# Row-major attention order, a new order of the mixing steps, and GELU as one operation

## The chip, the cores and the metric

One core of a Trainium2 chip runs the whole kernel. The metric is the device time of one execution in microseconds (us), as the median of several runs. The engines of the core are TensorE (PE, with its weight loads shown apart as PEld), VectorE (DVE), ScalarE (ACT), GpSimd (POOL) and SyncE (SP), which issues the DMAs.

## What is computed

Two layers of an encoder over 512 tokens, which form a grid of 8 rows and 64 columns, with 1024 channels in float32:

```python
h = rmsnorm(x, g_mix[l]); z = h @ w_in[l]                  # 1024 -> 2560
q, k, v, x_rec, gate = split(z)                            # 512 channels each
att = neighbourhood_attention(q, k, v, rel_bias[l])        # 8 heads of 64
xc = depthwise_conv(x_rec, width 4)
rec = (rg_lru(xc, forward) + rg_lru(xc, backward)) * gelu(gate, approximate=True)
x = x + concat(rmsnorm(att), rmsnorm(rec)) @ w_out[l]
h = rmsnorm(x, g_ffn[l]); a, b = split(h @ w_up[l])        # 1024 -> 2 x 3072
x = x + (gelu(depthwise_conv(a, width 3)) * b) @ w_down[l] # then, at the end, a last rmsnorm
```

In the attention each token sees all 8 rows and a window of 16 columns around its own column, clamped at the grid's edge, with a learned bias for each relative offset, and a softmax over these 128 keys. `rg_lru` has two gate products per direction (64x64 blocks), a decay exp(-8 r softplus(-lam)) and a linear scan over the tokens.

## The kernel before

Activations lie with channels on the 128 partitions and the 512 tokens along the free dimension. Each float32 matrix product is made of three passes over halves that are rounded to fp32r (`mm3`, L187 to L190): hi x hi, lo x hi, hi x lo. Weights arrive in chunks of 128x1024 (L157); ACT makes the hi half (L171), DVE the lo half (L172), three chunks ahead of their use. A column of the input projection, 128 output channels, is 24 matmuls of 128x512 (`column_parts`, L209).

A layer has a mixing stage and an MLP stage. The mixing stage begins with the four tiles of `x_rec` (L442) and then follows the list MIX (L43), whose steps are: q, k, v, g, one column of the projection with its evacuation (query_tile, key_tile, value_tile, gate_tile), where a and b are its halves; c, the convolution of a tile; t, the gate products of a tile with decay and scans (`lru_gates`, 12 matmuls and a long chain on ACT and DVE); u, the transposes of a value tile to token order, with copies of it moved by 64 partitions that POOL writes to `edge` (L564); S, T, P for each pair of heads and half of the grid's columns; o, parts of the output projection; n, the statistics of both norms. S, T and P have numbers 0 to 7: number n is head pair n // 2 and column half n % 2.

S (`scores`, L603) multiplies four blocks of queries, each 8 grid columns by 8 rows for two heads, with the keys of 16 or 24 grid columns: four float32 matmuls into two PSUM banks, then the bias and the maximum (L622), exp with its sum (L628) and the division (L632). T (`transposes`, L639) turns the probabilities into two banks and splits them in hi and lo (L653, L654). P (`products`, L657) multiplies by the values into one bank and copies the result into `att` (L679).

The program's text gives every instruction a place. The framework's scheduler then orders each engine's instructions: by modelled time it takes, of those that are ready, the one that stands first, and `with urgent()` (L141) moves instructions ahead of all that are not urgent. The order on each engine is fixed when the kernel is built. In the kernel before, scores and transposes are urgent as a whole (L724, L727), their matmuls too.

Tokens of a tile in attention stand in column order: by grid column, and the 8 rows of a column side by side. So a query, key or value tile is evacuated with a step of 8 elements on one side (L528, L536, L547), and the attention's result is copied back with a step of 64 (L679). A query tile is a pair of tiles, in each of which the part of the other head is zero (POOL, L517).

The pools that matter: `p_t` with 12 slots of 128x512 for most temporaries, `p_h` with 24, three PSUM banks for columns and gate products (`ps_mm`), two for scores (`ps_s`), two for transposes (`ps_pt`), one for products (`ps_o`; the fourth bank of a gate step until the first product has used it, L479).

Of the kernel before, what the change touches and what calls it, by code (L numbers as in the profile page):

```python
# [9 lines left out]
F32 = mybir.dt.float32  # L10
# [4 lines left out]
P = 128  # L15
# [24 lines left out]

MIX = ("q0 c0 c1 k0 t0 k1 q1 c2 t1 q2 k2 c3 t2 k3 q3 S0 v0a T0 t3 v0b g0a v1a S1 u0 P0 "  # L43
       "T1 g0b S2 v1b S3 g1a P1 u1 T2 v2a T3 P2 S4 S5 v2b g1b g2a T4 g2b P3 u2 P4 T5 S6 "
       "v3a v3b P5 g3a T6 S7 u3 o0 g3b P6 T7 o1 P7 o2 o3 o4 n o5 o6").split()
# [54 lines left out]
def encoder(ctx: ExitStack, tc: tile.TileContext, x_d, w_d, cols_d, bias_d, out_d):  # L100
# [153 lines left out]
    for t in edge:  # L254
        nc.gpsimd.memset(f32(t[0:64, 3 * P:T]), 0.0)
        nc.gpsimd.memset(f32(t[64:P, 0:P]), 0.0)

    NL = 16
    lam = cols[:, COLS["lru_lam"]:COLS["lru_lam"] + NL]
    sp = const.tile([P, NL], F32, name="sp")  # L260
# [79 lines left out]
    def by_column(ap):  # L340
        return ap.rearrange("p (c r) -> p r c", r=ROWS)

    def by_row(ap):
        return ap.rearrange("p (r c) -> p r c", r=ROWS)
# [82 lines left out]
    def layer(l, xn):  # L427
# [79 lines left out]
        qk = {}  # L507

        def query_tile(i):

            qk[i] = [big(p_h, "h", f"q{l}{i}{n}") for n in range(2)]

            def zones(other):
                return [by_head(t[64 * a:64 * a + 64])[:, :, a ^ other] for t in qk[i] for a in (0, 1)]

            for z in zones(1):
                nc.gpsimd.memset(z, 0.0)  # L517
            ps = psum(ps_mm, f"qps{l}{i}")
            yield from column_parts(ps, "w_in", l, i, xg, 4)
            with urgent():  # L520
                for n, z in enumerate(zones(0)):
                    rows = slice(64 * (n % 2), 64 * (n % 2) + 64)
                    cs = slice(32 * (n // 2), 32 * (n // 2) + 32)

                    def grid(ap):
                        return by_row(ap)[rows, :, cs].rearrange("p r (j c) -> p r j c", c=8)
# [12 lines left out]

        v = [None] * 4  # L540
# [29 lines left out]
        recs = [None] * 4  # L570
        atts = [None] * 4

        def gate_tile(t):
            ps = psum(ps_mm, f"gate{l}{t}")
            yield from column_parts(ps, "w_in", l, 16 + t, xg, 4)
            z = big(p_t, "t", f"z{l}{t}")
            with urgent():
                nc.vector.tensor_tensor(out=z, in0=ps, in1=rb, op=ALU.mult)
            s = big(p_t, "t", f"zs{l}{t}")
            nc.scalar.activation(s, z, AF.Square)  # L580
            nc.vector.tensor_scalar(out=s, in0=s, scalar1=0.044715, scalar2=1.0, op0=ALU.mult, op1=ALU.add)
            nc.vector.tensor_tensor(out=s, in0=s, in1=z, op=ALU.mult)
            nc.scalar.activation(s, s, AF.Tanh, scale=math.sqrt(2.0 / math.pi))
            nc.vector.scalar_tensor_tensor(out=z, in0=s, scalar=1.0, in1=z, op0=ALU.add, op1=ALU.mult)
            nc.vector.scalar_tensor_tensor(out=fb[t], in0=fb[t], scalar=0.5, in1=z, op0=ALU.mult, op1=ALU.mult)
# [16 lines left out]

        def scores(h):  # L603
            blocks = range(4 * (h % 2), 4 * (h % 2) + 4)
            bt, qt, kt = bias[h // 2], qk[h // 2][h % 2], qk[4 + h // 2]
            pr = {}
            st_ = probs_of[h % 2]
            mx = p_s.tile([P, 4], F32, tag="mx", name=f"mx{l}{h}")
            sm = p_s.tile([P, 4], F32, tag="sm", name=f"sm{l}{h}")
            for pair in (blocks[0:2], blocks[2:4]):  # L610
                ps = psum(ps_s, f"s{l}{h}{pair[0]}")
                o = 0
                for b in pair:
                    kc0, w, _ = BLOCKS[b]
                    nc.tensor.matmul(ps[:, o:o + ROWS * w], qt[:, b % 4 * P:(b % 4 + 1) * P],  # L615
                                     kt[:, ROWS * kc0:ROWS * (kc0 + w)], start=True, stop=True)
                    c0 = 0 if b % 2 else 2 * P - ROWS * w
                    pr[b] = st_[:, b % 4, c0:c0 + ROWS * w], ps[:, o:o + ROWS * w]
                    o += ROWS * w
                for b in pair:  # L620
                    _, w, bo = BLOCKS[b]
                    nc.vector.tensor_tensor_reduce(out=pr[b][0], in0=pr[b][1], in1=bt[:, bo:bo + ROWS * w], scale=1.0,  # L622
                                                   scalar=-3e38, op0=ALU.add, op1=ALU.max,
                                                   accum_out=mx[:, b % 4:b % 4 + 1])
                    pr[b] = pr[b][0]
            nc.vector.tensor_scalar(out=mx, in0=mx, scalar1=-1.0, scalar2=None, op0=ALU.mult)  # L626
            for b in blocks:
                nc.scalar.activation(pr[b], pr[b], AF.Exp, bias=mx[:, b % 4:b % 4 + 1],  # L628
                                     accum_out=sm[:, b % 4:b % 4 + 1])
            nc.vector.reciprocal(sm, sm)  # L630
            for b in blocks:
                nc.vector.tensor_scalar(out=pr[b], in0=pr[b], scalar1=sm[:, b % 4:b % 4 + 1], scalar2=None,  # L632
                                        op0=ALU.mult)
# [5 lines left out]
        def transposes(h, pr):  # L639
# [10 lines left out]
            sl = slice(n[0] * P, (n[-1] + 1) * P)  # L650
            t1, t2 = [[big(p_t, "t", f"pt{l}{h}{c}{a}", F32R) for a in range(2)] for c in range(2)]
            for t, src, cs in ((t1, whole, slice(0, T)), (t2, part, sl)):
                nc.scalar.activation(t[0][:, cs], src[:, cs], AF.Copy)  # L653
                nc.vector.tensor_tensor(out=t[1][:, cs], in0=src[:, cs], in1=f32(t[0][:, cs]), op=ALU.subtract)  # L654
            return t1, t2

        def products(h, t1, t2):  # L657
# [16 lines left out]
            at = att_t[0]  # L674
            for a in range(2):
                rows = slice(64 * a, 64 * a + 64)
                dst = by_row(at)[rows, :, 32 * (h % 2):32 * (h % 2) + 32].rearrange("p r (j c) -> p j c r", c=8)
                src = by_head(o)[rows, :, a].rearrange("p j (c r) -> p j c r", r=ROWS)
# [24 lines left out]
        for step in MIX:  # L703
# [128 lines left out]
def lay_out(inputs):  # L832
# [64 lines left out]
```

## Time and profile before

| | us |
|---|---|
| median of 3 runs (1231.11 to 1231.23) | 1231.18 |
| the profiled execution | 1230.33 |
| its span in the profile | 1228.5 |
| PE busy | 1201.5 (98%) |
| DVE busy | 791.6 (64%) |
| ACT busy | 488.0 (40%) |
| POOL busy | 46.3 (4%) |

The span is the time from the first to the last instruction of the program in the trace; the profiled execution's own time is 1.8 us longer. PE's granted clock is 0.998 of full speed over the span. A PE busy share counts from a matmul's start to its modelled end, and ends overlap with the next start, so the time that PE loses is read from starts. A row of waits says which engine and line waited, `<-` for what, then us in total, how often, and the longest.

### The profile page before, as it was taken

Reading aid. Unit: us, or ns where it says so; the run is one execution under the profiler, and the core shown is the slowest. Engines: PE = TensorE matmul, PEld = TensorE weight load, DVE = VectorE, ACT = ScalarE, POOL = GpSimd, SP = SyncE. Lnnn points to the kernel's source line nnn. Section 1 sums busy time; section 2 is a strip of 40 time slices with the busy share of each in tenths; the row PEclk is TensorE's granted clock in tenths of the full one; section 3 lists DMA queues with packets and bytes.
Section 4 is the critical chain, followed back from the end, with each engine's and each line's share of the span. In section 5 each row is a group of like instructions: output and inputs, shape, how many; then the busy total and the mean of one; then the engine's idle time right before and its main releaser. Section 6 shows DMA issues by size and latency. Waiting matters only on the chain.

```text
span 1228.5 us, 14279 instructions
## 1 busy us (share of the span) xinstructions
PE 1201.5 (98%) x5566; PEld 991.2 (81%) x5566; DVE 791.6 (64%) x1257; ACT 488.0 (40%) x717; POOL 46.3 (4%) x88
## 2 busy tenths in 40 slices
PE   9999999999999999999999999999999999999997
PEld 7777778888888888888887777788888888888886
DVE  8999876865544455553659998677555255565454
ACT  6687534433221232332429765344323212223220
POOL 2001010000000000000010011100000000000000
PEclk9999999999999999999999999999999999999999
DMA  7222213223223223233222221142332322322322
GB/s 239 81 69 93 84 35 103 90 99 103 91 98 103 87 101 103 88 102 103 86 86 77 77 86 52 35 137 87 103 93 96 103 91 98 103 87 101 103 69 69
DMA packets 34355, 114.06 MB, mean 93 GB/s; under 512 B 3825, under 2 KB 7025, under 8 KB 34289
## 3 DMA queue, kind: packets, MB, share of 16 engines
q1 hardware_dynamic: 34144, 113.17, 28.1%
q8 instruction: 43, 0.70, 0.2%
q14 instruction: 24, 0.19, 0.0%
q10 hardware_dynamic: 144, 0.00, 0.0%
HBM read 111.06 MB, written 2.10 MB: 92 GB/s over the span
## 4 chain that ended last, share of the span: by engine, by line
PE 78%; DVE 11%; ACT 4%; issue 2%; DMA 1%; POOL 0%; POOLq 0%; DVEq 0%; ACTq 0%
PE dn L188 7%; PE dn L190 7%; PE dn L189 7%; PE pl L188 6%; PE pa L188 6%; PE pa L189 6%; PE pl L189 6%; PE pa L190 6%; PE pl L190 6%; PE out L188 2%; PE out L190 2%; PE out L189 2%; DVE lo L172 2%; PE up L188 1%; PE up L190 1%
## 5 line engine op out<-in xcount | busy, mean ns | idle before, releaser
L171 ACT ACTIVATE hi<-raw 128x1024 fp32r<-128x1024 f32 (+1 forms) x205 | 216.3, 1055 | 452.9 <-PE dn L189 156.6
L172 DVE TENSOR_TENSOR lo<-raw,hi 128x1024 fp32r<-128x1024 f32 (+1 forms) x205 | 249.6, 1218 | 142.9 <-ACT hi L171 142.4
L763 DVE TENSOR_TENSOR ua<-pa,g_ffn_rb 128x512 f32<-128x512 f32 x44 | 30.4, 691 | 112.9 <-PE pa L190 112.9
L771 ACT ACTIVATE uc<-uc,cols 128x512 f32<-128x512 f32 x48 | 34.8, 724 | 129.7 <-DVE uc L769 129.6
L772 DVE TENSOR_TENSOR uc<-pl,uc 128x512 f32<-128x512 f32 x44 | 30.4, 691 | 73.5 <-PE pl L190 72.0
L740 DVE TENSOR_TENSOR dns<-dn,g_ffn_rb 128x512 f32<-128x512 f32 x30 | 20.4, 689 | 29.4 <-PE dn L190 29.4
L769 DVE SCALAR_TENSOR_TENSOR uc<-ua,cols,uc 128x511 f32<-128x511 f32 x48 | 36.0, 751 | 1.5
L767 DVE SCALAR_TENSOR_TENSOR uc<-ua,cols,uc 128x511 f32<-128x511 f32 x48 | 35.8, 745 | 0.1
L628 ACT ACTIVATE prob<-prob,mx 128x192 f32<-128x192 f32 (+1 forms) x64 | 27.5, 431 | 12.0 <-DVE mx L626 11.9
L615 PEld LDWEIGHTS s<-k,q 128*128 128x128 f32 x128 | 19.6, 190 | 8.8 <-issue 4.2
L188 PE MATMUL out<-atth,hi 128*128 128x512 f32 x64 | 26.1, 407 | 0.4 <-ACT atth L684 0.4
L615 PE MATMUL s<-k,q 128*128 128x192 f32 (+1 forms) x128 | 23.2, 324 | 3.2 <-DVE mx L622 1.4
L190 PE MATMUL out<-atth,lo 128*128 128x512 f32 x64 | 25.4, 397 | 0.0
L189 PE MATMUL out<-attl,hi 128*128 128x512 f32 x64 | 25.3, 396 | 0.0
L766 DVE TENSOR_SCALAR uc<-ua,cols 128x512 f32<-128x512 f32 x48 | 23.4, 487 | 1.5
L517 POOL MEMSET q<- 64x256 f32 x32 | 10.0, 311 | 367.4 <-PE dn L189 366.1
L679 DVE COPY att<-o 64x256 f32<-64x256 f32 x32 | 19.6, 612 | 4.6 <-PE o L190 4.1
L528 DVE TENSOR_TENSOR q<-qps,g_mix_rb 64x256 f32<-64x256 f32 x32 | 20.6, 644 | 0.4
L741 DVE TENSOR_TENSOR x<-x,dns 128x512 f32<-128x512 f32 x30 | 20.1, 687 | 0.4
L622 DVE CUSTOM_DVE_ANT_0 prob<-s,bias 128x192 f32<-128x192 f32 (+1 forms) x64 | 18.2, 338 | 1.8 <-PE pte L649 0.6
L564 POOL CAST edge<-vh 64x384 fp32r<-64x384 f32 x16 | 9.4, 591 | 254.5 <-ACT vh L559 254.0
L458 DVE SCALAR_TENSOR_TENSOR xc<-xrs,cols,xc 128x511 f32<-128x511 f32 (+1 forms) x24 | 17.9, 747 | 0.4
(930 smaller groups left out, 3547.4 us busy)
## 6 DMA issues: line engine op xcount, KB each, us to landing
raw<-in_w SPq DMA_DIRECT2D x203, 512.0 KB, 3.5
x<-in_x SPq DMA_DIRECT2D x8, 256.0 KB, 5.1
out_y<-out SPq DMA_DIRECT2D x8, 256.0 KB, 2.3
bias<-in_bias SPq DMA_DIRECT2D x8, 224.0 KB, 2.5
raw<-in_w SPq DMA_DIRECT2D x2, 256.0 KB, 3.1
cols<-in_cols SPq DMA_DIRECT2D x1, 164.0 KB, 5.0
cols<-in_cols ACTq DMA_DIRECT2D x1, 4.0 KB, 3.0
```

Source lines behind the costliest of these rows:

```text
L171: nc.scalar.activation(hi[:, sl], raw[:, sl], AF.Copy)
L172: nc.vector.tensor_tensor(out=lo[:, sl], in0=raw[:, sl], in1=f32(hi[:, sl]), op=ALU.subtract)
L188: nc.tensor.matmul(ps, a[0], b[0], start=start, stop=False)
L189: nc.tensor.matmul(ps, a[0], b[1], start=False, stop=False)
L190: nc.tensor.matmul(ps, a[1], b[0], start=False, stop=stop)
L615: nc.tensor.matmul(ps[:, o:o + ROWS * w], qt[:, b % 4 * P:(b % 4 + 1) * P], kt[:, ROWS * kc0:ROWS * (kc0 + w)], start=True, stop=True)
L628: nc.scalar.activation(pr[b], pr[b], AF.Exp, bias=mx[:, b % 4:b % 4 + 1], accum_out=sm[:, b % 4:b % 4 + 1])
L763: nc.vector.tensor_tensor(out=ua, in0=pa, in1=rbf[0], op=ALU.mult)
L767: nc.vector.scalar_tensor_tensor(out=c[:, 1:], in0=ua[:, :T - 1], scalar=w[0], in1=c[:, 1:], op0=ALU.mult, op1=ALU.add)
L769: nc.vector.scalar_tensor_tensor(out=c[:, :T - 1], in0=ua[:, 1:], scalar=w[2], in1=c[:, :T - 1], op0=ALU.mult, op1=ALU.add)
L771: nc.scalar.activation(c, c, AF.Gelu_apprx_tanh, bias=col("conv_ffn_b", j, l))
L772: nc.vector.tensor_tensor(out=c, in0=pl_, in1=c, op=ALU.mult)
```

## The change

- Attention's order of tokens. Keys are kept in the grid's own row-major order (plain evacuation), and the score matmul reads them through a view (`by_group`): groups of 8 grid columns, in them 8 rows, in them 8 neighbouring tokens. Queries and values are written in that order of groups, in runs of 8 tokens. The bias is laid out on the host to match.
- One query tile `q_pair` for all heads and both layers, whose zero parts are written once at the start, instead of a new pair of tiles with four memsets each time.
- A new MIX. The first two gate steps, the first scores and the first value tile come earlier; scores, transposes and products stand apart, with a column or half of one or a gate step between them.
- Urgency is taken from the matmuls of S and T and kept for what DVE and ACT do after them, and given to the copy of a product's result.
- The gate branch: GELU was written out with Square, Tanh and four DVE operations. Now `gate_tile` only evacuates, and a new step e makes one Gelu on ACT and one product on DVE.
- `p_t` has 10 slots instead of 12.

The diff, without the host's bias layout:

```diff
-MIX = ("q0 c0 c1 k0 t0 k1 q1 c2 t1 q2 k2 c3 t2 k3 q3 S0 v0a T0 t3 v0b g0a v1a S1 u0 P0 "
-       "T1 g0b S2 v1b S3 g1a P1 u1 T2 v2a T3 P2 S4 S5 v2b g1b g2a T4 g2b P3 u2 P4 T5 S6 "
-       "v3a v3b P5 g3a T6 S7 u3 o0 g3b P6 T7 o1 P7 o2 o3 o4 n o5 o6").split()
+MIX = ("q0 c0 k0 c1 t0 S0 c2 v0 t1 c3 u0 S1 q1 T0 k1 P0 S2 t2 v1a T1 v1b P1 u1 S3 q2 T2 k2 P2 S4 t3 v2a T3 v2b "
+       "P3 u2 S5 q3 T4 k3 P4 S6 v3 T5 g0 P5 u3 S7 g1 T6 e0 e1 g2 P6 e2 g3 T7 e3 o0 o1 P7 o2 o3 o4 n o5 o6").split()
...
-    p_t = pool("p_t", 12)
+    p_t = pool("p_t", 10)
...
+    q_pair = const.tile([P, 8, 2, 64], F32, name="q_pair")
+    nc.gpsimd.memset(q_pair[64:P, :, 0], 0.0)
+    nc.gpsimd.memset(q_pair[0:64, :, 1], 0.0)
...
+    def by_group(ap):
+        return ap.rearrange("p (r g c) -> p g r c", r=ROWS, c=8)
+    def in_group(ap):
+        return ap.rearrange("p g (r c) -> p g r c", r=ROWS)
...
         def query_tile(i):
...
             with urgent():
-                for n, z in enumerate(zones(0)):
-                    rows = slice(64 * (n % 2), 64 * (n % 2) + 64)
-                    cs = slice(32 * (n // 2), 32 * (n // 2) + 32)
...
-                    nc.vector.tensor_tensor(out=z.rearrange("p j (c r) -> p r j c", r=ROWS), in0=grid(ps),
-                                            in1=grid(rb), op=ALU.mult)
+                for n in range(2):
+                    rows = slice(64 * n, 64 * n + 64)
+                    nc.vector.tensor_tensor(out=in_group(q_pair[rows, :, n]), in0=by_group(ps)[rows],
+                                            in1=by_group(rb)[rows], op=ALU.mult)
         def key_tile(i):
...
-                nc.vector.scalar_tensor_tensor(out=by_column(qk[4 + i]), in0=by_row(ps), scalar=0.125,
-                                               in1=by_row(rb), op0=ALU.mult, op1=ALU.mult)
+                nc.vector.scalar_tensor_tensor(out=qk[4 + i], in0=ps, scalar=0.125, in1=rb, op0=ALU.mult, op1=ALU.mult)
         def value_tile(i):
...
-                nc.vector.tensor_tensor(out=by_column(o), in0=by_row(ps), in1=by_row(rb), op=ALU.mult)
+                nc.vector.tensor_tensor(out=in_group(o.rearrange("p (g n) -> p g n", g=8)), in0=by_group(ps),
+                                        in1=by_group(rb), op=ALU.mult)
...
+        def gate_end(t):
+            z = branch[t]
+            nc.scalar.activation(z, z, AF.Gelu_apprx_tanh)
+            nc.vector.tensor_tensor(out=fb[t], in0=fb[t], in1=z, op=ALU.mult)
             rec_stats.add(fb[t])
...
         def scores(h):
-                    nc.tensor.matmul(ps[:, o:o + ROWS * w], qt[:, b % 4 * P:(b % 4 + 1) * P],
-                                     kt[:, ROWS * kc0:ROWS * (kc0 + w)], start=True, stop=True)
+                    nc.tensor.matmul(ps[:, o:o + ROWS * w], q_pair[:, b], kt[:, kc0 // 8:(kc0 + w) // 8],
+                                     start=True, stop=True)
...
         def products(h, t1, t2):
-                nc.vector.tensor_copy(dst, src)
+                with urgent():
+                    nc.vector.tensor_copy(by_group(at)[rows, 4 * (h % 2):4 * (h % 2) + 4],
+                                          by_head(o)[rows, :, a].rearrange("p j (r c) -> p j r c", r=ROWS))
...
+            elif what == "e":
+                gate_end(n)
...
-                with urgent():
-                    probs[n] = scores(n)
+                probs[n] = scores(n)
             elif what == "T":
-                with urgent():
-                    turned[n] = transposes(n, probs.pop(n))
+                turned[n] = transposes(n, probs.pop(n))
```

## Rows read from the trace of the kernel before

**Rows 1.** The page: busy time of each engine, and one group of the MLP.

```profile
PE 1201.5 (98%) x5566; PEld 991.2 (81%) x5566; DVE 791.6 (64%) x1257; ACT 488.0 (40%) x717; POOL 46.3 (4%) x88
...
L763 DVE TENSOR_TENSOR ua<-pa,g_ffn_rb 128x512 f32<-128x512 f32 x44 | 30.4, 691 | 112.9 <-PE pa L190 112.9
```

**Rows 2.** Windows: stretch and its length, busy us of each engine, clock, DMA.

```profile
28.50:181.00 152.50, 144.07 (x709) 115.70 (x709) 138.66 (x283) 95.72 (x177) 10.23 (x16) 1.00 0.24 76
75.00:90.00 15.00, 13.46 (x60) 10.33 (x59) 14.97 (x21) 13.21 (x18) 0.00 (x0) 1.00 0.24 76
629.00:786.00 157.00, 148.43 (x734) 119.73 (x733) 139.64 (x280) 97.81 (x179) 15.52 (x29) 1.00 0.22 71
900.00:1000.00 100.00, 100.00 (x443) 82.81 (x442) 48.96 (x61) 27.17 (x30) 0.00 (x0) 1.00 0.30 97
```

**Rows 3.** Timeline of PE in the first mixing stage: start, us, instructions, idle before.

```profile
28.89 0.50 PE L188 MATMUL qps<-xg_g_mix_0h,hi 128*128 128x512 f32 x1 [0.26 <-DVE xrs L450]
...
46.41 1.46 PE L615 MATMUL s<-k,q 128*128 128x192 f32 x8
47.63 0.48 PE L190 MATMUL kps<-xg_g_mix_1h,lo 128*128 128x512 f32 x1
...
145.70 0.28 PE L188 MATMUL o<-pt,vh 128*128 128x256 f32 x1
...
147.04 0.29 PE L555 MATMUL vtp<-ident,vt 128*128 128x128 f32 x1
147.77 0.66 PE L645 MATMUL ptw<-ident,prob 128*128 128x128 f32 x4 [0.45 <-DVE pt L654]
148.27 0.49 PE L555 MATMUL vtp<-ident,vt 128*128 128x128 f32 x3
...
181.40 0.24 PE L322 MATMUL stats<-ones,rec_acc 128*128 128x1 f32 x1
```

**Rows 4.** Waits of PE's weight loader, 28.8 to 181.5 us.

```profile
PEld ptw L645 <- DVE pt L654: 3.5, 4, 1.9
PEld s L615 <- issue: 2.3, 2, 1.3
PEld o L190 <- POOL edge L564: 2.2, 4, 1.3
PEld s L615 <- DVE mx L622: 1.3, 4, 0.4
...
PEld gp L188 <- ACT w L483: 0.7, 2, 0.4
...
PEld ptw L645 <- DVE prob L632: 0.2, 1, 0.2
```

**Rows 5.** Groups of DVE, 28.5 to 181 us: busy us, mean ns | idle before.

```profile
L528 DVE TENSOR_TENSOR q<-qps,g_mix_rb 64x256 f32<-64x256 f32 x16 | 10.3, 642 | 0.2
L679 DVE COPY att<-o 64x256 f32<-64x256 f32 x16 | 9.8, 612 | 2.3 <-PE o L190 2.1
L622 DVE CUSTOM_DVE_ANT_0 prob<-s,bias 128x192 f32<-128x192 f32 x24 | 7.3, 354 | 0.0
...
L497 DVE TENSOR_TENSOR ti<-ti,w 128x512 f32<-128x512 f32 x8 | 5.6, 719 | 1.7 <-ACT w L495 1.7
L654 DVE TENSOR_TENSOR pt<-ptw,pt 128x512 fp32r<-128x512 f32 x8 | 5.5, 686 | 0.5 <-PE o L189 0.4
...
L547 DVE TENSOR_TENSOR vt<-vps,g_mix_rb 128x512 f32<-128x512 f32 x4 | 4.7, 1171 | 0.4 <-PE vps L190 0.4
L536 DVE SCALAR_TENSOR_TENSOR k<-kps,g_mix_rb 128x512 f32<-128x512 f32 x4 | 4.5, 1134 | 0.0
...
L582 DVE TENSOR_TENSOR zs<-zs,z 128x512 f32<-128x512 f32 x4 | 2.7, 686 | 0.1
```

**Rows 6.** Groups of ACT, 28.5 to 181 us.

```profile
L653 ACT ACTIVATE pt<-ptw 128x512 fp32r<-128x512 f32 x8 | 4.6, 580 | 0.0
...
L628 ACT ACT_TABLE_LOAD x2 | 2.6, 1283 | 2.0 <-DVE mx L626 2.0
```

More of the change, by code (lines that the diff above doesn't have):

```diff
@@ L337, in rows @@
             return r
[L340 to L344, printed above, removed]
+    def by_group(ap):
+        return ap.rearrange("p (r g c) -> p g r c", r=ROWS, c=8)
+    def in_group(ap):
+        return ap.rearrange("p g (r c) -> p g r c", r=ROWS)
     def by_head(ap):
@@ L509, in query_tile @@
         def query_tile(i):
[L511 to L517, printed above, removed]
             ps = psum(ps_mm, f"qps{l}{i}")
@@ L520, in query_tile @@
             with urgent():
-                for n, z in enumerate(zones(0)):
-                    rows = slice(64 * (n % 2), 64 * (n % 2) + 64)
-                    cs = slice(32 * (n // 2), 32 * (n // 2) + 32)
-                    def grid(ap):
-                        return by_row(ap)[rows, :, cs].rearrange("p r (j c) -> p r j c", c=8)
-                    nc.vector.tensor_tensor(out=z.rearrange("p j (c r) -> p r j c", r=ROWS), in0=grid(ps),
-                                            in1=grid(rb), op=ALU.mult)
+                for n in range(2):
+                    rows = slice(64 * n, 64 * n + 64)
+                    nc.vector.tensor_tensor(out=in_group(q_pair[rows, :, n]), in0=by_group(ps)[rows],
+                                            in1=by_group(rb)[rows], op=ALU.mult)
         def key_tile(i):
@@ L571, in layer @@
         atts = [None] * 4
+        branch = [None] * 4
         def gate_tile(t):
@@ L575, in gate_tile @@
             yield from column_parts(ps, "w_in", l, 16 + t, xg, 4)
-            z = big(p_t, "t", f"z{l}{t}")
+            branch[t] = big(p_t, "t", f"z{l}{t}")
             with urgent():
[L578 to L585, printed above, removed]
+                nc.vector.tensor_tensor(out=branch[t], in0=ps, in1=rb, op=ALU.mult)
+        def gate_end(t):
+            z = branch[t]
+            nc.scalar.activation(z, z, AF.Gelu_apprx_tanh)
+            nc.vector.tensor_tensor(out=fb[t], in0=fb[t], in1=z, op=ALU.mult)
             rec_stats.add(fb[t])
@@ L604, in scores @@
             blocks = range(4 * (h % 2), 4 * (h % 2) + 4)
-            bt, qt, kt = bias[h // 2], qk[h // 2][h % 2], qk[4 + h // 2]
+            bt, kt = bias[h // 2], by_group(qk[4 + h // 2])
             pr = {}
@@ L621, in scores @@
                     _, w, bo = BLOCKS[b]
-                    nc.vector.tensor_tensor_reduce(out=pr[b][0], in0=pr[b][1], in1=bt[:, bo:bo + ROWS * w], scale=1.0,
-                                                   scalar=-3e38, op0=ALU.add, op1=ALU.max,
-                                                   accum_out=mx[:, b % 4:b % 4 + 1])
+                    with urgent():
+                        nc.vector.tensor_tensor_reduce(out=pr[b][0], in0=pr[b][1], in1=bt[:, bo:bo + ROWS * w],
+                                                       scale=1.0, scalar=-3e38, op0=ALU.add, op1=ALU.max,
+                                                       accum_out=mx[:, b % 4:b % 4 + 1])
                     pr[b] = pr[b][0]
[L626 to L633, printed above, removed]
+            with urgent():
+                nc.vector.tensor_scalar(out=mx, in0=mx, scalar1=-1.0, scalar2=None, op0=ALU.mult)
+                for b in blocks:
+                    nc.scalar.activation(pr[b], pr[b], AF.Exp, bias=mx[:, b % 4:b % 4 + 1],
+                                         accum_out=sm[:, b % 4:b % 4 + 1])
+                nc.vector.reciprocal(sm, sm)
+                for b in blocks:
+                    nc.vector.tensor_scalar(out=pr[b], in0=pr[b], scalar1=sm[:, b % 4:b % 4 + 1], scalar2=None,
+                                            op0=ALU.mult)
             return st_
@@ L652, in transposes @@
             for t, src, cs in ((t1, whole, slice(0, T)), (t2, part, sl)):
-                nc.scalar.activation(t[0][:, cs], src[:, cs], AF.Copy)
-                nc.vector.tensor_tensor(out=t[1][:, cs], in0=src[:, cs], in1=f32(t[0][:, cs]), op=ALU.subtract)
+                with urgent():
+                    nc.scalar.activation(t[0][:, cs], src[:, cs], AF.Copy)
+                    nc.vector.tensor_tensor(out=t[1][:, cs], in0=src[:, cs], in1=f32(t[0][:, cs]), op=ALU.subtract)
             return t1, t2
@@ L676, in products @@
                 rows = slice(64 * a, 64 * a + 64)
-                dst = by_row(at)[rows, :, 32 * (h % 2):32 * (h % 2) + 32].rearrange("p r (j c) -> p j c r", c=8)
-                src = by_head(o)[rows, :, a].rearrange("p j (c r) -> p j c r", r=ROWS)
-                nc.vector.tensor_copy(dst, src)
+                with urgent():
+                    nc.vector.tensor_copy(by_group(at)[rows, 4 * (h % 2):4 * (h % 2) + 4],
+                                          by_head(o)[rows, :, a].rearrange("p j (r c) -> p j r c", r=ROWS))
             if h % 2:
@@ L867, in lay_out @@
     rel = a["rel_bias"]
-    bias = np.full((L, H, 8, ROWS, NBIAS), MASKED, np.float32)
+    bias = np.full((L, H, ROWS, 8, NBIAS), MASKED, np.float32)
     for q0, (kc0, w, bo) in ((0, BLOCKS[0]), (8, BLOCKS[1]), (56, BLOCKS[7])):
-        part = bias[..., bo:bo + ROWS * w].reshape(L, H, 8, ROWS, w, ROWS)
+        part = np.full((L, H, ROWS, 8, ROWS, w), MASKED, np.float32)
         for qr in range(ROWS):
@@ L874, in lay_out @@
                 s = min(max(qc - 8, 0), GW - 16)
-                win = rel[:, :, 7 - qr:15 - qr, s - qc + 15:s - qc + 31]
-                part[:, :, c, qr, s - kc0:s - kc0 + 16, :] = win.transpose(0, 1, 3, 2)
-        bias[..., bo:bo + ROWS * w] = part.reshape(L, H, 8, ROWS, ROWS * w)
+                part[:, :, qr, c, :, s - kc0:s - kc0 + 16] = rel[:, :, 7 - qr:15 - qr, s - qc + 15:s - qc + 31]
+        part = part.reshape(L, H, ROWS, 8, ROWS, w // 8, 8).transpose(0, 1, 2, 3, 5, 4, 6)
+        bias[..., bo:bo + ROWS * w] = part.reshape(L, H, ROWS, 8, ROWS * w)
     bias = bias.reshape(L, H // 2, P, NBIAS)
```

## The prediction

> **What bounds the kernel now.** I read the page first: TensorE (PE) is busy 1201.5 of 1228.5 us, VectorE (DVE) 64% [rows 1]. A PE share of 98% says that only PE's own work and its waits count, but busy ends are modelled, so I then compared stretches. In the windows, a stretch of the MLP (900 to 1000 us) takes 443 matmuls in 100 us, 0.226 us each, with PE never idle and DVE half idle. The stretch of the mixing stage is different: in 28.5:181 DVE is busy 138.7 of 152.5 us (91%), in 75:90 it is full (14.97 of 15) while PE has 1.5 us of plain idle, and the second layer (629:786) looks alike [rows 2]. So outside the two mixing stages nothing is to be had, and inside them PE and DVE are close to each other.
>
> How much PE waits there I get from PE's timeline, by starts and not by busy ends. The stage runs from the first query matmul at 28.89 to the first stats matmul at 181.40: 152.5 us. Its work: 384 column matmuls, 48 of the gates and 45 of the output steps, 477 x 0.226 = 107.7 us; 8 score groups, each 1.22 us (46.41 to the next start at 47.63), 9.8 us; 8 product groups of 1.34 us (145.70 to 147.04), 10.7 us; 56 transposes of probabilities and 16 of values at 0.125 us (four from 147.77 to 148.27), 7.0 + 2.0 us [rows 3]. Sum 137.2 us, so 15.3 us of each stage are waits, 30.6 us in the two layers. That is the most that any new order can give: 1231.2 - 30.6 = 1200.6.
>
> The waits of PE's weight loader name them: 21 groups between 28.8 and 181.5 sum to 19.5 us, from 3.5 down to 0.2 [rows 4]. They are in front of loads, some of which hide behind a running matmul; so I count each by 15.3/19.5 = 0.785.
>
> **The change part by part.** *DVE work removed.* Query evacuation: four 642 ns operations of 64x256 become two of 64x512 whose both sides run in eights; key 1134 and value 1171 ns are written at a step of 8 elements now, and become plain or runs of 8; the copies of att (612 ns, 16 a layer) too [rows 5]. A plain 128x512 operation that reads PSUM takes 691 ns [rows 1]. No row shows the new forms. Bounds: the plain rate below, today's rate per element above. I take the plain rate, since the queries already read PSUM in runs of 8 and what slows these rows is the step inside the run. Per layer: 4 x (2.57 - 1.38) = 4.8, 4 x 0.44 = 1.8, 4 x 0.48 = 1.9, and for the copies, an estimate of 0.2 each, 3.2: 11.7 us. GELU as one operation takes out three DVE operations of up to 686 ns [rows 5], 1.8 us a gate, 7.2 a layer, and one ScalarE (ACT) pass. So DVE falls from 138.7 to about 120 us beside 137 of PE work. This time is not on the path by itself; it shortens the waits. If the runs of 8 give nothing, DVE still falls to 131.
>
> *GELU's table.* Gelu needs another ACT table than Exp, and a load of one costs 1.28 us [rows 6]. The MLP's first Gelu loads it anyway; if the order puts a gelu between two heads' exponentials, two or three more loads, 4 us a layer, go to ACT, which is busy 95.7 of 152.5 us [rows 2]. Their cover is the 15 us or more of PE work between a head's scores and its transposes in the new order; I cost them at nothing, 1 us a layer at most.
>
> *The new order and the urgency.* PE's instructions of scores and transposes lose their precedence and stand where MIX puts them; only the DVE and ACT work behind them keeps it. Between two heads' transposes there are now at least 11 us of PE work, between two products at least 10 (a column 5.4, a gate step 2.7, a score group 1.2). What that takes away, in loader waits per layer:
> - transposes waiting for the previous ones to be split (DVE pt, prob), three groups, 4.4 us, the first 3.5 [rows 4]: all.
> - scores, 4.5 us in three groups, two of which stand in [rows 4]: 1.3 us for a bank of the previous head go; of 2.3 us without a releaser I count half, as they stand in front of hoisted matmuls; 0.9 us for the key stays, since S2, S4 and S6 stand one product (1.34 us) behind their key tile. 2.5 us go.
> - products, 5.2 us in six groups, the largest the 2.2 us for POOL's edge copies [rows 4]: the edge copies now come a whole column or more ahead, and the one product bank is free long before. 3.9 us go, 1.3 for the split probabilities stay.
> - output steps on atth and attl, 0.9 us: go, as they come after all their inputs.
> Together 11.7 x 0.785 = 9.2 us a layer. What stays: gate products and next columns on the Tanh or the key that empties their bank, 2.2 us in all (0.7 the largest group [rows 4]).
>
> *What is late next.* P1 and P3 stand half a value tile (12 matmuls, 2.7 us) behind T1 and T3. Their split is 0.58 + 0.69 on ACT and DVE, then 0.48 and 0.55 in part beside it [rows 5, 6], 1.8 to 2.3 us, and an operation under way on DVE in front of it (0.6 us on the mean): 2.7 us is just not enough, 0.3 us each. u1 and u2 stand one product (1.34 us) behind their value tile, whose evacuation takes 0.7 us and the same queueing: 0.2 each. I take 1.0 us a layer; the bounds are 0 (the scheduler fills the gap with the ready scores) and 4 x 1.2.
>
> *One query tile.* All heads share q_pair, so q1 to q3 can only be written once the scores of the heads before have read it; the order has S1, S3, S5 right ahead of q1, q2, q3, 5.4 us of column before the write. Nothing waits. The 16 POOL memsets per layer go; POOL was idle 93% of the stage [rows 2].
>
> *Keys read in runs.* The moving operand of the scores becomes runs of 8 keys with hops of 64 elements. No matmul of the trace reads with gaps. Lower end: no change. Upper end, by the nearest rows, DVE's operations that hop: 1134 against 691 ns, 1.64 times [rows 1, 5], so 0.64 x 9.8 = 6.3 us a layer. I take no change, as those rows hop at every element and this one at every eighth.
>
> [...]
>
> *Smaller pool.* p_t has 10 slots instead of 12. In the MLP a tile pair is in work for a few us of 10.9, so it is covered. In the mix it may not be (rival D).
>
> Sum: 9.2 - 1.0 = 8.2 us a layer, 16.4 in both. The profiled execution took 1230.3 (span 1228.5 and 1.8 around it); the median of the runs is 1231.2, 0.9 above. 1231.2 - 16.4 = 1214.8; I say 1215.
>
> **The rivals.** *B, nearly clean:* with DVE at 120 of 137 us the Tanh waits shrink too and only 3 us of waits are left a layer: 2 x 12.3, 1206.6. For it: nearly all waits have DVE in them. Against: DVE's load is not even.
>
> *C, DVE stays full in the first half:* until 105 us the new order wants two more heads' scores (8 bias operations of 354 ns [rows 5] with their normalisations, 3.3 us a head), a transpose split 1.2, three products' copies and splits 3.6, three value tiles 3.5, 14.9 us in all, and gives back one query and one key tile, 3.7, and 5 of faster forms: 6 us more (estimates from the same durations) in a stretch where DVE is already full. That the scheduler, which orders by readiness as modelled, hoists again belongs here. Half to all of the 6 us stands on PE: the gain falls to between 5.1 and 2 us a layer, 1221 to 1227, say 1224.
>
> *D, slots:* t1 and t2 come 9 us earlier than now, and T1 wants four p_t slots while t1 and t2 hold up to ten. A gate step's DVE work is 7.4 us (six groups from L497's 719 ns up to the two scans) [rows 5]; if T's copies wait half of that, 3.7 us, at three places a layer and PE's three column banks fill behind it, that is 22 us: 1231.2 - 18.4 + 22 = 1235, slower. It turns the sign from 3.1 us a place on. For it: scans are not urgent and DVE is full there. Against: columns that need no slot are ready on PE at all times.
>
> *E, keys in runs cost:* the score groups take 1.64 times, 12.6 us in both layers: 1227.4. From 1.84 times on the change is not faster. [...]
>
> **How the numbers follow.** Forecast 0.50 (its own range 1208 to 1221), B 0.15, C 0.20, E 0.06, D 0.09. 1205 to 1229 leaves out a third of B, most of D and some of C and E, 0.17. A measurement of this kernel can tell 0.2%, 2.5 us. Faster (under 1228.7): forecast, B, 0.17 of C, 0.03 of E, 0.85. Same: 0.03 of C, 0.02 of E, 0.01 of D, 0.06. Slower: 0.08 of D, 0.01 of E, 0.09.
>
> **What would show it.** Right: from the first query matmul to the first stats matmul about 144 us; DVE in that stretch about 120 us; the query operation near 0.69 us, key and value too; loader waits on DVE pt, POOL edge and DVE att gone; a score group still 1.2 us. Wrong: waits on pt copies that begin with a slot of p_t (D), PE's waits on keys, queries and Tanh larger than now (C), score matmuls with a wider pace (E), a stage over 150 us.

## The result, and the profile after

The changed kernel takes 1239.72 us, the median of 4 runs (1239.11 to 1241.28), against 1231.2 before: the ratio is 1.0071, with an interval from 1.0054 to 1.0089. It is slower by 0.7%; the forecast of 1215 was 24.7 us too low, and its range ended at 1229.

The page of the changed kernel, first its busy times, then one group of its list:

```profile
PE 1199.3 (97%) x5566; PEld 1001.0 (81%) x5566; DVE 758.0 (61%) x1217; ACT 487.7 (39%) x713; POOL 38.1 (3%) x58
...
L547 PE MATMUL vtp<-ident,vt 128*128 128x128 f32 x32 | 5.9, 316 | 20.8 <-DVE vt L538 19.0
```

DVE has 33.6 us less work than in [rows 1], and the kernel is slower. The second row says where: 32 transposes of value tiles, 5.9 us of work, have 20.8 us of idle PE in front of them. The span is 9.4 us longer than before.

DVE's new forms, from 28.5 to 186 us (busy us, mean ns):

```profile
L673 DVE COPY att<-o 64x256 f32<-64x256 f32 x16 | 6.7, 420 | 4.1 <-PE o L190 4.0
L520 DVE TENSOR_TENSOR q_pair<-qps,g_mix_rb 64x512 f32<-64x512 f32 x8 | 5.5, 688 | 2.6 <-PE qps L190 2.5
...
L538 DVE TENSOR_TENSOR vt<-vps,g_mix_rb 128x512 f32<-128x512 f32 x4 | 2.7, 687 | 0.8 <-PE vps L190 0.7
L528 DVE SCALAR_TENSOR_TENSOR k<-kps,g_mix_rb 128x512 f32<-128x512 f32 x4 | 2.7, 684 | 2.2 <-PE kps L190 2.2
```

Beside [rows 5], the copies fell from 612 to 420 ns, the value from 1171 to 687, the key from 1134 to 684, all as forecast. Windows of the changed kernel, the whole stage and two stretches in it:

```profile
28.50:186.00 157.50, 143.95 (x717) 120.64 (x716) 123.81 (x266) 98.31 (x178) 10.76 (x16) 0.97 0.23 73
...
60.00:62.00 2.00, 0.03 (x1) 0.06 (x2) 2.00 (x6) 2.00 (x4) 0.00 (x0) 0.50 0.00 0
62.00:65.00 3.00, 3.00 (x10) 2.51 (x11) 3.00 (x5) 3.00 (x6) 0.00 (x0) 0.50 0.00 0
```

DVE's stage fell from 138.7 us [rows 2] to 123.8. But from 60 to 62 us PE does nothing while DVE and ACT are full. PE's timeline shows the stage's ends and this hole (start, us, instructions, idle before):

```profile
29.16 0.50 PE L188 MATMUL qps<-xg_g_mix_0h,hi 128*128 128x512 f32 x1
...
42.91 1.36 PE L607 MATMUL s<-k,q_pair 128*128 128x128 f32 x8
43.97 0.52 PE L188 MATMUL vps<-xg_g_mix_0h,hi 128*128 128x512 f32 x1
...
54.20 0.49 PE L643 MATMUL pte<-ident,prob 128*128 128x128 f32 x3
61.97 1.08 PE L547 MATMUL vtp<-ident,vt 128*128 128x128 f32 x4 [7.27 <-DVE vt L538]
62.70 0.77 PE L188 MATMUL qps<-xg_g_mix_0h,hi 128*128 128x512 f32 x1
63.28 0.63 PE L189 MATMUL qps<-xg_g_mix_0l,hi 128*128 128x512 f32 x1
63.70 0.63 PE L190 MATMUL qps<-xg_g_mix_0h,lo 128*128 128x512 f32 x1
...
185.64 0.28 PE L327 MATMUL stats<-ones,rec_acc 128*128 128x1 f32 x2
```

The stage takes 156.5 us; before it was 152.5 [rows 3]. With the prediction's 137.2 us of work, 19.3 us are waits and slower matmuls (15.3 before). At 61.97 the transposes of value tile 0 (step u0) begin after 7.27 us of idle PE; in the second layer that hole is 9.08 us. S1 and T0, which stand behind u0 in MIX, had run ahead of it (T0's last transposes at 54.20), and the column of q1 stands behind u0 in PE's order.

A group of scores takes 1.06 us (42.91 to 43.97), not more than the 1.22 of [rows 3]. With plain keys 1.06 us occurs as well, so keys read in runs neither cost nor gain; PE in the kernel before:

```profile
92.52 1.36 PE L615 MATMUL s<-k,q 128*128 128x128 f32 x8
93.58 0.53 PE L188 MATMUL qps<-xg_g_mix_7h,hi 128*128 128x512 f32 x1
```

The five longest groups of waits of PE's weight loader up to 186 us:

```profile
PEld vtp L547 <- ACT ti L488: 7.5, 1, 7.5
PEld vtp L547 <- ACT a L491: 3.0, 2, 1.7
PEld o L190 <- POOL edge L556: 1.8, 4, 0.8
PEld o L190 <- DVE vl L552: 1.5, 1, 1.5
PEld s L607 <- DVE k L528: 1.5, 1, 1.5
```

The waits on split probabilities and on mx, which were 3.5 and 1.3 us in [rows 4], are gone, as forecast. Those on POOL's edge copies, which were to go too, are still 1.8 us (2.2 before). In place of what is gone stands u0. The loader's row names ACT's Tanh, but PE's timeline names the evacuation vt, which ended last. Why was it so late? Its column was done at about 49.6 us. This is DVE's timeline from there:

```profile
49.66 0.54 DVE L460 TENSOR_SCALAR xc<-xrs,cols 128x512 f32<-128x512 f32 x1
50.11 0.68 DVE L495 SCALAR_TENSOR_TENSOR w<-a,w 128x512 f32<-128x512 f32 x1
50.71 0.74 DVE L463 SCALAR_TENSOR_TENSOR xc<-xrs,cols,xc 128x510 f32<-128x510 f32 x1
51.38 1.22 DVE L172 TENSOR_TENSOR lo<-raw,hi 128x1024 fp32r<-128x1024 f32 x1
...
53.17 0.68 DVE L496 SCALAR_TENSOR_TENSOR ti<-ti,xc 128x512 f32<-128x512 f32 x1
...
54.82 0.68 DVE L502 TENSOR_TENSOR ti<-ti,w 128x512 f32<-128x512 f32 x1
...
56.09 1.22 DVE L505 TENSOR_TENSOR_SCAN fb<-a,ti 128x512 f32<-128x512 f32 x1
57.23 1.20 DVE L508 TENSOR_TENSOR_SCAN w<-a,ti 128x512 f32<-128x512 f32 x1
...
59.07 0.66 DVE L510 TENSOR_TENSOR fb<-fb,w 128x512 f32<-128x512 f32 x1
59.65 0.97 DVE L626 TENSOR_SCALAR prob<-prob,sm 128x192 f32<-128x192 f32 x4
60.54 0.68 DVE L305 TENSOR_TENSOR xcs_2l<-xc,xcs_2h 128x512 fp32r<-128x512 f32 x1
61.14 0.68 DVE L538 TENSOR_TENSOR vt<-vps,g_mix_rb 128x512 f32<-128x512 f32 x1
```

DVE was never idle, and the urgent evacuation ran directly behind the last, not urgent operation of c2 (xcs_2l). In front of it stood c2, the rest of t0 with both scans, the softmax of S1 and the lo half of a weight chunk. Two theories follow. *Theory A, the row of slots:* the framework gives a pool's slots out in the program's order; c2 stands ahead of v0 in MIX and takes three slots of p_h, so the evacuation, which writes into p_h too, can't be placed before c2's operations. *Rival F, the load:* a gate step with its convolution is, from these rows, 2 x (0.68 + 0.68 + 0.68) + 1.22 + 1.20 + 0.66 = 7.2 and 0.54 + 3 x 0.74 + 0.68 = 3.4, together 10.6 us of DVE beside 2.7 of PE; a column is 1.22 + 0.68 = 1.9 of DVE beside 5.4 of PE. So a gate step (7.9 over) needs 2.3 columns (3.5 each) beside it. The old list has two between neighbouring gate steps; the new one has v0 alone between t0 and t1, and scores as well. The prediction's own rivals C (DVE full in the first half) and D (slots of p_t) remained too.

### The profile page after: what moved, and what is told of

Same layout as the page of the kernel before. It is cut to its first block, busy times and chain, and to the rows that moved or that the text cites. A ratio compares the mean times of both kernels' runs of the same rounds, so it can differ in the third digit from the quotient of the medians.

```text
span 1237.9 us, 14170 instructions
## 1 busy us (share of the span) xinstructions
PE 1199.3 (97%) x5566; PEld 1001.0 (81%) x5566; DVE 758.0 (61%) x1217; ACT 487.7 (39%) x713; POOL 38.1 (3%) x58
## 4 chain that ended last, share of the span: by engine, by line
PE 87%; DVE 7%; ACT 3%; issue 2%; POOL 0%; POOLq 0%; DVEq 0%; ACTq 0%
PE dn L189 7%; PE dn L188 7%; PE dn L190 7%; PE pl L189 6%; PE pa L189 6%; PE pa L190 6%; PE pl L190 6%; PE pl L188 6%; PE pa L188 6%; PE out L190 2%; PE out L188 2%; PE out L189 2%; PE xr L188 1%; PE up L188 1%; PE gate L190 1%
## 5 line engine op out<-in xcount | busy, mean ns | idle before, releaser
L547 PE MATMUL vtp<-ident,vt 128*128 128x128 f32 x32 | 5.9, 316 | 20.8 <-DVE vt L538 19.0
L607 PE MATMUL s<-k,q_pair 128*128 128x192 f32 (+1 forms) x128 | 23.3, 325 | 2.6 <-DVE k L528 2.6
L615 DVE CUSTOM_DVE_ANT_0 prob<-s,bias 128x192 f32<-128x192 f32 (+1 forms) x64 | 18.6, 335 | 10.9 <-PE s L607 10.7
L607 PEld LDWEIGHTS s<-k,q_pair 128*128 128x128 f32 x128 | 21.2, 196 | 3.8 <-DVE k L528 3.0
L547 PEld LDWEIGHTS vtp<-ident,vt 128*128 128x128 f32 x32 | 4.0, 160 | 22.8 <-ACT a L491 14.0
L673 DVE COPY att<-o 64x256 f32<-64x256 f32 x32 | 13.4, 420 | 8.3 <-PE o L190 8.1
L188 PE MATMUL pa<-xg_g_ffn_0h,hi 128*128 128x512 f32 x44 | 17.1, 389 | 0.0
```

Of the source, the lines that this page charges most:

```text
L188: nc.tensor.matmul(ps, a[0], b[0], start=start, stop=False)
L607: nc.tensor.matmul(ps[:, o:o + ROWS * w], q_pair[:, b], kt[:, kc0 // 8:(kc0 + w) // 8], start=True, stop=True)
```

## The experiments

**The row of slots.** Three ways round u0's wait, on the changed kernel: the value tiles in another pool, v0 ahead of c2, and u0 behind q1.

```diff
# vt_pt
-            o = big(p_h, "h", f"vt{l}{i}")
+            o = big(p_t, "t", f"vt{l}{i}")
# v0first
-... S0 c2 v0 t1 c3 u0 S1 q1 T0 ...
+... S0 v0 c2 t1 c3 u0 S1 q1 T0 ...
# u0late
-... S0 c2 v0 t1 c3 u0 S1 q1 T0 ...
+... S0 c2 v0 t1 c3 S1 q1 u0 T0 ...
```

> The new kernel with one word changed: the value tiles are written into slots of p_t instead of p_h; the list MIX and all else stay. In the changed kernel PE stands 7.3 and 9.1 us before the transposes of value tile 0, waiting for its evacuation, which stands on DVE right behind the last, not urgent operation of c2 although it is urgent. Theory A (the framework gives the slots of a pool out in program order, so the urgent evacuation can't be placed before c2 has taken its three slots of p_h): the evacuation comes before the second scores' softmax on DVE, PE's two waits shrink from 16.4 to under 2 us together and the slow matmuls behind them (about 3 us) go too, 1239.7 - 18 = 1222 (1218 to 1226). Theory C (DVE is full there, and what is moved ahead only pushes something else back): the waits on vt go, but waits of the same length appear at the next scores, keys or queries, 1235 to 1241. Theory D (p_t with 10 slots is too small): four more tiles in that pool make it worse, above 1240.

> The new kernel with two neighbours of MIX swapped, v0 ahead of c2. Theory A (slots in program order): the value tile asks for its slot before c2 does, so its evacuation moves forward on DVE as in the kernel with the value tiles in p_t; 1222 (1218 to 1226), with PE's wait for vt under 2 us in both layers together, and t2 perhaps a little later since c2 is. Theory C (DVE full): 1235 to 1241, waits at other places. Theory D (p_t too small): no change, 1238 to 1241.

> The new kernel with u0 moved behind S1 and q1 in MIX; DVE's order at that place stays, the evacuation of value tile 0 is as late as before. Theory A: PE does the 5.4 us of q1 in the time in which it stood, and the transposes of the values then come when the evacuation is just done: what is left is 7.5 - 5.4, 2 us in the first layer and about 4 in the second, 1239.7 - 10 - 2 (slow matmuls) = 1228 (1223 to 1231). Theory C (DVE full, PE waits for it wherever the steps stand): 1236 to 1241. Theory D: 1238 to 1241.

Measured: 1232.28 (1.0009, from 0.9999 to 1.0018), 1231.11 (0.9999, 0.9990 to 1.0009) and 1231.06 (0.9995, 0.9985 to 1.0004). In vt_pt the evacuation stands 24 instructions further ahead in DVE's trace, directly behind c2's first operation, and it runs 11 us earlier:

```profile
49.63 0.54 DVE L460 TENSOR_SCALAR xc<-xrs,cols 128x512 f32<-128x512 f32 x1
50.09 0.68 DVE L538 TENSOR_TENSOR vt<-vps,g_mix_rb 128x512 f32<-128x512 f32 x1
```

So it is shown that the pool held the evacuation back: only the pool was changed. With the pool kept and v0 ahead of c2 the evacuation runs as early (49.85 us), as a row in program order would have it. But each of the three gains 7.4 to 8.7 us, where A expected 18, 18 and 12 and C at most 5: neither accounts for it alone. What is late next, from vt_pt's waits of PE in the first and in the second layer:

```profile
PE o L188 <- ACT vh L551: 3.8, 1, 3.8
PE gp L188 <- ACT w L488: 2.7, 1, 2.7
...
PE o L188 <- ACT vh L551: 7.1, 1, 7.1
```

ACT's timeline with v0 ahead of c2 has vh behind the split of c3, which is ahead of u0 in MIX and waits 2.57 us for DVE. That vh stands there because of the row of p_h is argued from this, not shown:

```profile
72.93 0.63 ACT L304 ACTIVATE xcs_3h<-xc 128x512 fp32r<-128x512 f32 x1 [2.57 <-DVE xc L463]
73.47 1.04 ACT L171 ACTIVATE hi<-raw 128x1024 fp32r<-128x1024 f32 x1
74.41 0.58 ACT L551 ACTIVATE vh<-vtp 128x512 fp32r<-128x512 f32 x1
```

**More slots of p_t (rival D).** The tiles of x_rec go to p_h, and nothing else changes.

```diff
-            xr.append(big(p_t, "t", f"xrs{l}_{t}"))
+            xr.append(big(p_h, "h", f"xrs{l}_{t}"))
```

> The new kernel with the four tiles of x_rec in slots of p_h instead of p_t, so that the gate steps and the split probabilities have up to four more slots of p_t; MIX stays. Theory A (the evacuation of the value tile is held by the order of slots in p_h): PE's waits for vt stay at 19 us, 1238 to 1242. Theory D (p_t with 10 slots holds the gate steps and the transposes): most of the 25 us between forecast and result goes, under 1228.

Measured: 1240.46 (1.0077, from 1.0062 to 1.0092), no change, and PE's wait for vt stays (7.3 us at the longest in the first layer). Too few slots of p_t are not what holds this kernel.

**Out of both rows.** First c2 and c3 behind u0 and P0 in MIX; then MIX unchanged, vt of every tile in p_t as in vt_pt, and vh and vl of tile 0 there as well.

```diff
# convlate
-... S0 c2 v0 t1 c3 u0 S1 q1 T0 k1 P0 S2 t2 ...
+... S0 v0 t1 u0 c2 S1 q1 T0 k1 P0 c3 S2 t2 ...
# vtvh_pt, on vt_pt
-            hi = big(p_h, "h", f"vh{l}{i}", F32R)
-            lo = big(p_h, "h", f"vl{l}{i}", F32R)
+            hi = big(p_t if i == 0 else p_h, "t" if i == 0 else "h", f"vh{l}{i}", F32R)
+            lo = big(p_t if i == 0 else p_h, "t" if i == 0 else "h", f"vl{l}{i}", F32R)
```

> The new kernel with c2 and c3 moved in MIX behind u0 and P0: ... S0 v0 t1 u0 c2 S1 q1 T0 k1 P0 c3 S2 t2 ... With v0 merely ahead of c2 PE waited 3.0 and 7.1 us in front of the first product for the split of the transposed values (vh), which on ACT stands behind the split of c3, whose tiles ask for slots of p_h before it. Theory A (slots in program order): now both vt and vh come before c2 and c3, the waits for vt and vh go in both layers (10.1 us), and the slow matmuls behind them: 1231.1 - 12 = 1219 (1215 to 1224). Rival F (DVE and ACT are both full between 45 and 70 us, DVE 24.5 and ACT 24.3 of 25 us with v0 ahead of c2, so PE waits for them whatever is first): the waits move to the gate products of t2, to the Tanh that empties their banks or to keys, 1228 to 1234.

> The new kernel, MIX as it is, with the value tiles and the split transposed values of tile 0 in slots of p_t instead of p_h: the same work for every engine, only these slots don't stand in one row with those of c2 and c3. Theory A: the waits of the kernel with the value tiles alone in p_t for vh (3.8 and 7.1 us) shrink to under 2 us together, 1232.3 - 9 - 2 = 1221 (1217 to 1226). Rival F (DVE and ACT full at that place): those waits turn up at the Tanh that empties the banks of the gate products, 1229 to 1235. Theory D (p_t too small): the three more slots hold up the split probabilities, above 1235.

Measured: 1228.59 (0.9985, 0.9975 to 0.9995) and 1245.12 (1.0115, 1.0100 to 1.0130). A expected about 1220 of both and falls as a full account; F's 1228 to 1234 holds in convlate, and D's forecast, above 1235, in vtvh_pt. In convlate the wait moved to the gate products of t2, which wait for c2's split (PE's waits, first layer, then DVE, where that split runs behind t1's scans):

```profile
PE gp L189 <- DVE xcs_2l L305: 4.4, 1, 4.4
PE o L189 <- DVE pt L649: 2.1, 1, 2.1
```

```profile
73.06 1.20 DVE L508 TENSOR_TENSOR_SCAN w<-a,ti 128x512 f32<-128x512 f32 x1
74.18 0.67 DVE L305 TENSOR_TENSOR xcs_2l<-xc,xcs_2h 128x512 fp32r<-128x512 f32 x1
```

In vtvh_pt the added tiles bring rival D to life: ACT's split of the probabilities waits for a scan of DVE whose result it does not read, which leaves the slot as the link, and PE's products wait 10.9 us for the split probabilities in the second layer. First ACT's timeline, then PE's waits:

```profile
704.70 0.60 ACT L648 ACTIVATE pt<-ptw 128x512 fp32r<-128x512 f32 x1 [3.67 <-DVE w L508]
```

```profile
PE o L189 <- DVE pt L649: 10.9, 5, 6.8
```

**The parts alone, on the kernel before.** GELU as one operation; the token order; both; both with the change's urgency.

```diff
# b_gelu: the seven lines of GELU become
+            nc.scalar.activation(z, z, AF.Gelu_apprx_tanh)
+            nc.vector.tensor_tensor(out=fb[t], in0=fb[t], in1=z, op=ALU.mult)
# b_layout, of four such places
-                nc.vector.scalar_tensor_tensor(out=by_column(qk[4 + i]), in0=by_row(ps), scalar=0.125,
-                                               in1=by_row(rb), op0=ALU.mult, op1=ALU.mult)
+                nc.vector.scalar_tensor_tensor(out=qk[4 + i], in0=ps, scalar=0.125, in1=rb, op0=ALU.mult, op1=ALU.mult)
# b_both_urg, on both, of four such places
-                with urgent():
-                    probs[n] = scores(n)
+                probs[n] = scores(n)
```

> The kernel before with one edit: Gelu as one operation in the gate step. By the prediction's account DVE has 7.2 us less in each layer, but most of it in the second half, where PE waits little; ACT gets up to three more table loads a layer. 1228 to 1231 if the DVE time is not on the path, 1224 if it shortens the waits by its share of DVE's work (7.2 of 138.7, 0.8 us a layer, and the scores' and transposes' waits behind gate operations), over 1232 if table loads of 1.28 us delay the exponentials.

> The kernel before with the new order of tokens alone: keys plain, queries, values and the result in runs of 8, scores reading the keys through the view; MIX, urgency, pairs of query tiles with their memsets and GELU as before. If the faster forms (11.7 us of DVE a layer by the prediction's account) are worth something by themselves: 1224 to 1228; if the order of instructions alone decides PE's waits: 1229 to 1232; if the scores pay for keys in runs of 8 (rival E): 1237 or more.

> The kernel before with the new order of tokens and Gelu as one operation; MIX, urgency, query pairs and p_t's 12 slots as before. The two edits alone gave 12.5 and 5.0 us. If they add: 1231.0 - 17.5 = 1213.5 (1212 to 1215), and the loss of the whole change then lies in the new MIX and its urgency alone (about 26 us). If the waits that they shorten are partly the same ones: 1215 to 1218.

> The kernel with both edits on the old MIX, and the change's urgency: matmuls of scores and transposes not urgent, what DVE and ACT do behind them and the copy of a product's result urgent. If the urgency is what costs (PE takes columns ahead of scores and transposes, and these come late): 1220 or more. If it is the list MIX that costs: within 3 us of the kernel with both edits, 1211 to 1216.

Measured: 1225.88 (0.9959, 0.9944 to 0.9974), 1218.39 (0.9899, 0.9884 to 0.9914), 1214.27 (0.9863, 0.9847 to 0.9880) and 1211.24 (0.9838, 0.9823 to 0.9852). Each of these parts is a gain, and together they are below the forecast. The token order alone shortens the stage to 146.5 us (the ends of it in b_layout):

```profile
29.38 0.50 PE L188 MATMUL qps<-xg_g_mix_0h,hi 128*128 128x512 f32 x1
...
175.83 0.39 PE L322 MATMUL stats<-ones,rec_acc 128*128 128x1 f32 x3
```

**The old urgency with the new MIX.**

```diff
-                probs[n] = scores(n)
+                with urgent():
+                    probs[n] = scores(n)
```

(and the same for the transposes)

> The whole change with the old urgency: scores and transposes urgent as a whole, their matmuls too; MIX as changed. If the urgency is what costs: under 1222. If MIX is what costs, by giving DVE and ACT more work up to about 70 us than the columns beside it cover: 1236 to 1243, with PE's wait for the value tile still over 5 us in each layer.

Measured: 1243.65 (1.0108, 1.0092 to 1.0123). The copy of a product's result stays urgent here. The urgency is a gain of 3 to 4 us with either list; MIX is the loss.

**Less work of DVE, the order kept.** On convlate, where c2 and c3 no longer stand ahead of vt and vh. This kernel leaves out the reverse direction's last product, its scan and the sum of both directions:

```diff
             for d, a, w, ti in work:
-                nc.vector.tensor_tensor(out=ti, in0=ti, in1=w, op=ALU.mult)
                 if d == 0:
+                    nc.vector.tensor_tensor(out=ti, in0=ti, in1=w, op=ALU.mult)
...
-                else:
-                    nc.vector.tensor_tensor_scan(out=w[:, ::-1], data0=a[:, ::-1], data1=ti[:, ::-1], initial=0.0,
-                                                 op0=ALU.mult, op1=ALU.add)
-                    nc.vector.tensor_tensor(out=fb[t], in0=fb[t], in1=w, op=ALU.add)
```

> The kernel with c2 and c3 moved back, without the reverse direction's last product, its scan and the sum of both directions (these results are left out): 0.686 + 1.20 + 0.747 = 2.63 us less DVE work a gate step, 10.5 us a layer, half of it before the third gate step; the order of steps stays. Rival F (between 45 and 90 us DVE has more work than PE's columns cover, and PE waits for the excess): the waits shrink by 4 to 8 us a layer, 1228.6 - 8 to - 16 = 1212 to 1221. Theory A alone (only the row of slots held things up, and it is cured here): 1226 to 1229, as the scans aren't urgent and stand behind what PE waits for.

Measured: 1210.54 (0.9833, 0.9818 to 0.9848): 18.05 us less than convlate, for 21 us of DVE work less, none of it urgent. F expected 8 to 16, A alone at most 3, so F's mechanism holds and its price was too low. The span's mean granted clock rose with it, from 0.992 to 0.998, so part of the gain may be the clock's; how much is not shown. One stretch from 60 to 75 us, in convlate and in lessscan:

```profile
60.00:75.00 15.00, 8.54 (x47) 6.86 (x45) 14.85 (x25) 10.45 (x14) 0.00 (x0) 0.98 0.21 70
```

```profile
60.00:75.00 15.00, 14.36 (x75) 11.87 (x74) 14.88 (x32) 13.56 (x25) 0.00 (x0) 1.00 0.21 71
```

DVE is full in both; with less to do it lets PE run 75 matmuls in place of 47. ACT, with the same work, isn't the limit. What is left out also frees slots of p_t sooner; the runs don't tell that apart, but convlate's longest wait, for xcs_2l, needs no such slot.

**The gate steps spread again.** The whole change with other lists, and the ten slots alone.

```diff
# balA (its rest as in the change, g0 to g3 earlier)
+q0 c0 k0 c1 t0 k1 v0 c2 t1 u0 k2 S0 k3 c3 S1 q1 t2 T0 v1a T1 v1b P0 S2 P1 u1 S3 q2 t3 T2 ...
# balB
+q0 c0 c1 k0 t0 k1 v0 c2 t1 k2 u0 k3 c3 S0 t2 v1 S1 q1 T0 t3 T1 v2a P0 S2 v2b P1 u1 S3 q2 T2 g0 ...
# urg_pt10, on b_both_urg
-    p_t = pool("p_t", 12)
+    p_t = pool("p_t", 10)
```

> As balB, but with the first attention steps nearer the front: two columns ahead of t0 and t1, three ahead of t2 but also S0 and S1, and two ahead of t3 with T0, T1, P0, P1, S2, S3. Theory F: what is saved in the first 60 us is there (no wait for the value tile), but the stretch around t3 has four heads' softmax work beside two columns: between balB and the kernel with c2 and c3 moved back, 1214 to 1224. If only the front matters: as balB within 2 us.

> The whole change (single query tile, ten slots, its urgency, its e steps) with another list: every gate step t0 to t3 has two columns ahead of it, and the attention from S1 on starts behind t2, most of it behind t3. Theory F (a gate step and its convolution are about 10.7 us of DVE beside 2.7 us of PE, a column 5.4 us of PE beside 1.9 of DVE; the changed list has one column between t0 and t1): PE's waits in the first layer's stage fall from 20 to under 9 us, 1209 to 1216. If the single query tile or the ten slots cost: 1222 or more.

> The kernel with the old list, both edits and the new urgency (1211.2), p_t with 10 slots instead of 12. If ten slots are enough: 1210 to 1213. If slots cost (rival D): 1216 or more, with waits on the split probabilities or the Tanh.

Measured: balA 1211.16 (0.9839, 0.9822 to 0.9855), balB 1210.65 (0.9834, 0.9819 to 0.9849), urg_pt10 1211.29 (0.9839, 0.9825 to 0.9854). Ten slots cost nothing on the old list, and the single query tile costs nothing that shows. balA came out better than F expected of it (1214 to 1224), within 2 us of balB: only the front mattered. Its stage, 142.5 us, and its window from 60 to 75 us:

```profile
28.67 0.39 PE L188 MATMUL qps<-xg_g_mix_0h,hi 128*128 128x512 f32 x1
...
171.20 0.39 PE L327 MATMUL stats<-ones,rec_acc 128*128 128x1 f32 x3
```

```profile
60.00:75.00 15.00, 15.00 (x72) 12.69 (x71) 13.54 (x34) 12.98 (x28) 2.01 (x4) 1.00 0.28 87
```

Both are versions of the change that beat the kernel before and the changed one. Neither clearly beats the old list with the same other parts (urg_pt10): a new order repaired the loss and gained nothing that shows.

## Why the prediction was wrong, step by step

- *The shares of the change, from the runs:* token order and GELU together -16.9 us, urgency -3.0, ten slots 0, the list MIX with the single query tile +28.4 (1211.29 to 1239.72). balA and balB, which keep that tile, put the last on the list. Of the 28.4 us, 11.1 went by moving c2 and c3 (convlate) and 17.4 more with the gate steps spread (balA).
- *The step that failed is "The new order and the urgency":* it credited order and urgency with 9.2 us of waits a layer. The urgency gave 3.0 us in both layers, the order cost 28.4 as written and gave nothing that shows in balA and balB. Most of these waits were waits for DVE time. On the old list, with no other order, the stage fell by 6.0 us by the token order alone (152.5 to 146.5) and by 8.0 with GELU as well (b_both, 29.00 to 173.47). "This time is not on the path by itself; it shortens the waits" was right, but I then booked the waits under the order.
- *"What is late next" left u0 out.* It weighed P1, P3, u1 and u2, 1.0 us a layer. I read how far u1 and u2 stood behind their tiles and did not follow v0 to u0, where c2, the rest of t0 and the softmax of S1 lay between on DVE: 7.27 and 9.08 us. By F's balance the list is 7.9 - 3.5 = 4.4 us short at t1, and 1.6 more for the softmax of a score step (1.33 + 0.16 + 0.17 + 0.97 on DVE at L615 to L626, less 1.06 of PE): 6.0 us, an estimate made after the result, beside 7.27 and 9.08 measured.
- *Rival C was the mechanism, mis-sized.* Its 6 us of too much DVE work a layer is of the size of the hole at u0, but it took them from a gain that the order didn't bring, and it ended at 1227. Behind u0 the same shortage turned up again at vh and c3 (v0first) and at t2 (convlate): the 17.4 us above.
- *The row of slots was in no rival.* Out of it, vt_pt gained 7.4 us, and convlate, with c2 and c3 out of the way, 11.1; both overlap with F, in which a late place costs only where DVE has much to do, and convlate moves DVE work back as well. How much is the row's alone stays open.
- *Right:* the forms of DVE at the plain rate; the score groups (rival E is out: keys read from SBUF in runs of 8 show 1.06 us, and so do plain ones); GELU's table loads (11 in the changed kernel's stage for 8 before, 1283 ns each; b_gelu gained 5.0 us); the smaller pool, and D's mechanism where more tiles enter it. The sum of PE's work took 1.22 us for each score group, the long end of what the kernel before shows; eight of 1.06 would make it 135.9 and the waits 16.6, which changes no step. "A stage over 150 us" was named as a sign that the prediction is wrong.

## What to carry to other kernels

A new order of steps is weighed step by step as a balance: what each step asks of the second engine, and what the steps beside it cover; a sum over half a stage hides a local shortage, and PE, with q1 behind u0 in its order, paid it here with 7.27 us of standing. An urgent instruction was only as early as its output slot (another pool brought vt forward by 11 us): look which other tiles of its pool stand ahead of it in the program. When several edits come together, the faster forms can be measured on the old order first, which shows whose waits they were.

## What the hardware showed that I had not expected

After standing 7.27 us PE ran at about half its pace: the granted clock was 0.50 from 60 to 65 us in the windows of the changed kernel, and q1's matmuls start 0.42 us apart (63.28, 63.70) against 0.226 in the MLP [rows 2]. About twelve of them do so, from 62.70 to 67.90 us: 5.2 us in place of 2.7, 2.5 on top of the wait. So this wait cost more than itself. The mean granted clock of the span was 0.989 against 0.998 before, and 0.998 again in balA and balB.
